# A hybrid attention and recurrence layer: shifting and centring the recurrent values through memory and with tokens on partitions, in place of 128 small products per run, and storing the last results block by block

## The chip, the cores and the metric

The kernel runs on one core of a Trainium2 chip. The metric is the device time of one execution in microseconds (us). Before the change it is 1977.34 us, the median of three runs between 1976.89 and 1977.49 us. The engines are named as the profile names them: PE is TensorE with its matrix products, PEld its weight loads, DVE is VectorE, ACT is ScalarE, POOL is GpSimd, SP is SyncE, whose queue issues nearly all transfers.

## What is computed

The layer projects 256 tokens of width 4096 once, and feeds two groups of heads and a gate from the result:

```python
proj = jnp.einsum('bsd,dc->bsc', x, w_in)
...
rw = rw_cols.astype(f32)
rw_prev = jnp.pad(rw, ((0, 0), (1, 0), (0, 0)))[:, :-1]
rw = rw + (rw_prev - rw) * mu_shift.astype(f32)
r, kr, vr, wd, ad = jnp.split(rw, _split_points(IN_SIZES[4:9]), axis=-1)
...
y = _rwkv7_scan(rh, decay.reshape(hs), kh, vh, -kk, kk * ah)
mu = jnp.mean(y, axis=-1, keepdims=True)
var = jnp.mean(jnp.square(y - mu), axis=-1, keepdims=True)
y = ((y - mu) * lax.rsqrt(var + GN_EPS)).reshape(B, S, RWKV_WIDTH) * gn_gain + gn_bias
bonus = jnp.sum(rh * kh * r_k, axis=-1, keepdims=True) * vh
rwkv_out = y + bonus.reshape(B, S, RWKV_WIDTH)

h = jnp.concatenate([fox_out, rwkv_out], axis=-1) * jax.nn.silu(z.astype(f32))
out = jnp.einsum('bsc,cd->bsd', h.astype(x.dtype), w_out)
x = _layernorm(ALPHA * x.astype(f32) + out.astype(f32), ln_gain, ln_bias, LN_EPS).astype(x.dtype)
```

The change is about `vr`, the values of the recurrence. Each of their 2048 columns is mixed with the same column one token earlier (the token shift). The scan writes `v_t k_t^T` into a state and reads that state, so its output is linear in the values. The kernel uses that: the mean over the 64 columns of a head, which the normalisation of `y` takes away, is taken away from the values ahead of the scan.

## The kernel before, in words

**Blocks.** The recurrent and attention heads are worked in eight pairs n, each of two groups of 128 columns. A pair has four blocks b of 512 projection columns. A block is 16 pieces of 512 KB of weights (`w_n_b_q`), and each piece is 12 products with 128x128 stationary and 128x512 moving operands: every float32 operand is split in a rounded part "h" and a rest "l", and three products are made of each (`mm`, L147 to L149). `fetch` (L214 to L218) issues the load of a piece on SP into one of four raw buffers `w`; ACT casts it to "h" (L141), DVE subtracts to get "l" (L142). There are four "h" buffers and three "l" buffers.

**What runs beside them.** All other work is written as generators, advanced by `slot` after every second step of a block. Code order thus sets the order of PE; for the other engines a scheduler orders the instructions by what it believes of their times, and each engine then runs its own list strictly in order. A wait of one instruction holds up all that stand behind it on its engine.

**The values.** Block b = 1 of a pair holds the values of the recurrence (256 columns of each of the two token halves m) and those of the attention. ACT copies the first to the tile `bk` (L807). `unload` turns them with products against the identity (`tr`, L722), so that columns lie on partitions and tokens run along the row; there the shift by one token is a shift along the row (`shifted`, `lerp`, L268 and L269), giving the tile `s2`, called `v` in `rwkv`. `rwkv` needs them the other way round again, with tokens on partitions, 64 to a chunk, and centred: L488 to L496 multiply `v` by the matrix `cent`, which turns and centres at once, into `vp`. ACT copies `vp` to the tiles `SV` and `UV` (L521, L522). `v` also goes into the bonus (`bon`, L524).

**What follows in a pair.** `gp` (L487) are the products of keys and queries of the chunks, masked by DVE to `gb` and `lt` (L507, L515). `gb` goes through memory (`nd`, L510) and comes back spread over all partitions (`Nb`, L511). Then DVE solves 32 small triangular systems row by row (L543, L546, tiles `prod` and `xc`), whose result goes through memory again (`td`, `T`, L552 to L554) and is turned into `X` (L559); only then come the products that read `SV` and `UV` (L575 onwards). POOL scales the keys by the chunk's decay (L490).

**The end.** After the last block of the output projection, the second token half is normalised block by block on DVE (L913) and on ACT (L944), and `store` (L907) issues the transfers of the result: two of two blocks each, then four of one block each.

Of the kernel before, what the change touches and what calls it, by code (L numbers as in the profile page):

```python
# [10 lines left out]
F32 = mybir.dt.float32  # L11
BF16 = mybir.dt.bfloat16
F32R = mybir.dt.float32r
AF = mybir.ActivationFunctionType
ALU = mybir.AluOpType
AX = mybir.AxisListType

P = 128
# [33 lines left out]
C_ID = 0  # L52
C_MASK = 128
C_ONES = 256
C_CENT = 384
C_E = 512
C_SCAN = 640
C_ROW = C_SCAN + S
C_W = C_ROW + 2
# [3 lines left out]
def constants():  # L63
    p = np.arange(P)[:, None]
    s = p % C
    t = np.arange(C)[None, :]
    cst = np.zeros((P, C_W), np.float32)
    cst[:, C_ID : C_ID + P] = np.eye(P)
    cst[:, C_MASK : C_MASK + C] = s < t
    cst[:, C_MASK + C : C_MASK + 2 * C] = s <= t  # L70
    same = (np.arange(P)[:, None] // HD) == (np.arange(P)[None, :] // HD)
    cst[:, C_ONES : C_ONES + P] = same
    cst[:, C_CENT : C_CENT + P] = np.eye(P) - same / HD
    j = (p % NG) * NJ + np.arange(P)[None, :] // B
    cst[:, C_E : C_E + P] = j == np.arange(P)[None, :] % B
    cst[:, C_SCAN : C_SCAN + S] = (np.arange(S)[None, :] % C) != 0
    first = np.array([1, 1, 0, 1, 0, 1], np.float32)
    sign = np.array([-1, -1, -1, 1, 1, 1], np.float32)
    cst[:6, C_ROW] = sign * (2 * first - 1)
    cst[:6, C_ROW + 1] = sign * (1 - first)  # L80
    return cst


@with_exitstack
def layer(ctx: ExitStack, tc: tile.TileContext, xt, xtok, w_lora, w_main, w_o, up, par, mulora, fbias, lng, lnb, cst, out):
    nc = tc.nc
    PS = bass.MemoryType.PSUM

# [6 lines left out]
    def pst(name):  # L95
        return ps.tile([P, 512], F32, tag="ps", name=name)
# [33 lines left out]

    ident = cs[:, C_ID : C_ID + P]
    ones = cs[:, C_ONES : C_ONES + P]
    cent = cs[:, C_CENT : C_CENT + P]

    def column(name, i):
        return prm[:, PAR.index(name), i : i + 1]
# [55 lines left out]
    def wait(n):  # L192
        for _ in range(n):
            yield
# [182 lines left out]
        return t.rearrange("p a b -> p (a b)")  # L377

    rk = {}
    pairs = {}  # L380
    done = set()
    prepared = set()
# [92 lines left out]
    def rwkv(n):  # L475
# [12 lines left out]
        v = vv[n]  # L488
        kept = BK[:, :, 0 : NCH - 1, :]
        nc.gpsimd.tensor_tensor(kept, kept, lc[:, :, 0 : NCH - 1].unsqueeze(3).to_broadcast([P, 2, NCH - 1, P]), ALU.mult)  # L490
        vp = pst(f"vp{n}")
        for u in range(2):
            for c in range(NCH):
                for j in range(2):
                    h, o = HALF[j], HALF[1 - j]
                    nc.tensor.matmul(vp[o, u * S + c * C : u * S + (c + 1) * C], v[:, u, c * C : (c + 1) * C], cent[:, h], start=True, stop=True)  # L496

        def m(rows):
            return cs[rows, C_MASK : C_MASK + P].unsqueeze(1).to_broadcast([C, NCH, P])

# [14 lines left out]
                nc.vector.tensor_tensor(lt[j][o, u], gv[u][j][o], m(o), ALU.mult)  # L515
        SV = [rp.tile([P, 2, NCH, C], F32, tag=f"SV{j}", name=f"SV{j}_{n}") for j in range(2)]
        UV = [rp.tile([P, 2, NCH, C], F32, tag=f"UV{j}", name=f"UV{j}_{n}") for j in range(2)]
        for j in range(2):
            o = HALF[1 - j]
            vo = vp.rearrange("p (u c t) -> p u c t", u=2, t=C)[o]  # L520
            nc.scalar.copy(SV[j][o], vo)  # L521
            nc.scalar.copy(UV[j][o], vo)  # L522
            nc.gpsimd.memset(SV[j][HALF[j], :, 0, :], 0.0)
        nc.vector.tensor_tensor(flat(bon), flat(bon), flat(v), ALU.mult)  # L524
        for u in range(2):
            nc.scalar.activation(bon[:, u], bon[:, u], AF.Identity, bias=column("gn_bias", i0 + u))
# [24 lines left out]
        for u in range(2):  # L551
            nc.sync.dma_start(out=td[u].rearrange("q c (g j) s -> (q c g) (j s)", g=NG), in_=flat(xc[:, u]))  # L552
            for a in range(4):
                nc.sync.dma_start(out=T[B * a : B * (a + 1), u], in_=td[u, a].rearrange("c r s -> r c s"))  # L554
        yield from wait(W["d2"])
        for a in range(4):
            o = C * (a // 2) + B * (a % 2)
            rows = slice(B * a, B * (a + 1))
# [146 lines left out]

    unloading = []

    def unload(n, b, bk, vt):
        yield from wait(LAG)
        if b == 0:  # L710
            while n and 2 * n - 1 not in prepared:
                yield
        elif b == 2:
            while n and n - 1 not in done:
                yield
        fq = fk = None
        cols = BLOCKS[b]
        for h in range(len(cols) // 2):
            tr = pst(f"tr{n}_{b}_{h}")
            for t in range(2):  # L720
                for m in range(2):
                    nc.tensor.transpose(tr[:, t * S + m * P : t * S + (m + 1) * P], bk[:, m, (2 * h + t) * P : (2 * h + t + 1) * P], ident)  # L722
            for t in range(2):
                p = tr[:, t * S : (t + 1) * S]
                j, u = cols[2 * h + t]
                i = 2 * n + u
                if j < 3:
                    rk[i, j] = shifted(p, j, i)
                elif j == 3:
                    while i and i - 1 not in foxed:  # L730
                        yield
                    fq = t256("fq", f"fq{i}")
                    nc.scalar.mul(fq, p, FOX_SCALE)
                elif j == 4:
                    fk = t256("fk", f"fk{i}")
                    nc.scalar.copy(fk, p)
                    side(fox(i, fq, fk, vt))
                else:
                    silu2(p, f"fr"[j - 5] + str(i))
            yield  # L740
        unloading.clear()
# [57 lines left out]
    for n in range(G // 2):  # L799
        for b in range(4):  # L800
            acc = block(n, b)
            while unloading:
                slot()
            bk = rp.tile([P, 2, OB], F32, tag="bk", name=f"bk{n}_{b}")
            for m in range(2):
                if b == 1:
                    nc.scalar.copy(bk[:, m, : 2 * P], acc[m][:, : 2 * P])  # L807
                else:
                    nc.scalar.copy(bk[:, m, :], acc[m])
            if b == 1:  # L810
                while n and 2 * n - 1 not in foxed:
                    slot()
                vt = rp.tile([P, 2, 2 * P], F32, tag="vt", name=f"vt{n}")
                for m in range(2):
                    nc.scalar.copy(vt[:, m, :], acc[m][:, 2 * P :])
            unloading.append(n)
            side(unload(n, b, bk, vt))
# [3 lines left out]
    for b, q in outs:  # L821
        if q == 0:
            pool, tag = (ps, "ps") if b == 1 or b and b % 2 == 0 else (pp, "pp")
            oacc[b] = [pool.tile([P, 512], F32, tag=tag, name=f"oacc{b}_{m}") for m in range(2)]
        acc = oacc[b]
        hi, lo = weights(f"wo{b}_{q}")
        for j in range(2):
            k = 2 * q + j
            if b < 2 and q < CUT:
                slot()  # L830
                if b == 0 and k + KT - BACK < FAR:
                    get_h(k + KT - BACK)
            while k not in ht:
                slot()
            if b > 1 and k == 4:
                load_tok(b)
            for m in range(2):
                if m and b == NB - 1 and q >= KT // 2 - LATE:
                    late.append((k, j, hi, lo))
                else:  # L840
                    project(acc[m], k, j, m, hi, lo)
        if q < KT // 2 - 1:
            continue
        if b == 0:
            while sides:
                slot()
            mid.close()
            rpool = ctx.enter_context(tc.tile_pool(name="rpool", bufs=1))
            res = [rpool.tile([P, D], F32, tag=f"res{m}", name=f"res{m}") for m in range(2)]
            rows = rpool.tile([P, D], F32R, name="rows")  # L850
            nc.gpsimd.memset(rows.bitcast(F32), 0.0)
            identr = const.tile([P, P], F32R, name="identr")
            nc.vector.tensor_copy(identr, ident)
            for n in range(2):
                load_tok(n)
            lneps = const.tile([P, 1], F32, name="lneps")
            nc.vector.memset(lneps, LN_EPS)
        if b < NB - 1:
            for m in range(2):
                add(m, b)  # L860
            for m in range(2):
                gain(m, b)
# [42 lines left out]
    def store(m, b, n):  # L905
        o = slice(b * OB, (b + n) * OB)
        nc.sync.dma_start(out=out[m * P : (m + 1) * P, o], in_=res[m][:, o])  # L907
# [31 lines left out]
    for n in range(HALVED):  # L939
        b = HALVED + n  # L940
        finish(1, b, l1, pp, "pp")
        o = slice(n * OB, (n + 1) * OB)
        nc.tensor.matmul(wps[n], la, rows[:, o], start=False, stop=True)
        nc.scalar.mul(res[1][:, o], wps[n], rss[1])  # L944
        if n == 1:
            store(1, 0, 2)
            store(1, HALVED, 2)
        elif n > 1:
            store(1, n, 1)
            store(1, b, 1)  # L950


def arrange(inputs):
# [12 lines left out]
    tiles = np.stack([t.reshape(KT, P, G // 2, 2, P) for t in types])  # L966
    main = np.stack([np.stack([tiles[j, :, :, :, u] for j, u in c], 3) for c in cols])
    res["w_main"] = np.ascontiguousarray(main.transpose(3, 0, 2, 1, 4, 5)).reshape(G // 2, 4, P, KT, OB)
    wo = a["w_out"].reshape(2, G, P, NB, OB)
    res["w_o"] = np.ascontiguousarray(wo.transpose(3, 2, 1, 0, 4).reshape(NB, P, KT, OB))  # L970
    res["up"] = np.ascontiguousarray(np.stack([a["w_up"].reshape(LORA, G, P).transpose(1, 0, 2), a["a_up"].reshape(LORA, G, P).transpose(1, 0, 2)], 2))
# [26 lines left out]
```

## Time and profile before

| what | value |
|---|---|
| median of three runs | 1977.34 us |
| the profiled execution's own time | 1977.29 us |
| its span in the trace | 1975.5 us |
| granted clock of PE over the span | 0.999 |
| PE, DVE, ACT, POOL busy | 99%, 67%, 51%, 2% |
| moved to and from memory | 387.64 MB, 196 GB/s |
| `vp` products in the trace | 256 records, 32 to a pair |
| POOL instructions | 86 |

The span is the time from the first to the last recorded instruction; the 1.8 us between it and the execution's own time lie outside the trace. Busy shares are averages over the span. Since one engine is busy nearly all of the time, the reading goes by that engine's list: what is taken off it, and what could make it wait.

### The profile page before, as it was taken

The numbers are of one execution on the slowest core, as the hardware profiler recorded it, in microseconds if no ns is written. First come the engines' busy times: TensorE is split into PE (matmuls) and PEld (weight loads), VectorE is DVE, ScalarE is ACT, GpSimd is POOL, SyncE is SP. The second block draws the span as 40 slices with busy tenths as digits, with TensorE's granted clock in tenths as the row PEclk, the third lists the DMA queues.
The fourth block names the chain that finished last, engine by engine and source line by source line (L and its number), as shares of the span: only waits on it lengthen the run. The fifth ranks groups of instructions, "written<-read, shape, count | busy, mean of one in ns | idle before, by whom it ended". The sixth has DMA issues, their size and how long they took to land.

```text
span 1975.5 us, 28732 instructions
## 1 busy us (share of the span) xinstructions
PE 1964.6 (99%) x10633; PEld 1615.7 (82%) x10633; DVE 1323.6 (67%) x2096; ACT 1007.9 (51%) x1525; POOL 37.7 (2%) x86
## 2 busy tenths in 40 slices
PE   9999999999999999999999999999999999999998
PEld 8888788878887888788878887888788878888886
DVE  6678576857685768576857685768576846755555
ACT  6554564456445644564456445644564444443332
POOL 0100000000000000000000000000000000000000
PEclk9999999999999999999999999999999999999999
DMA  9566566655665666566656665666566777866664
GB/s 336 150 198 179 178 191 199 189 166 192 199 185 169 193 193 187 173 193 192 184 177 192 198 186 170 190 195 189 171 186 184 244 281 235 253 199 201 190 202 161
DMA packets 140589, 387.64 MB, mean 196 GB/s; under 512 B 32224, under 2 KB 42480, under 8 KB 140448
## 3 DMA queue, kind: packets, MB, share of 16 engines
q1 hardware_dynamic: 140016, 385.38, 64.7%
q8 instruction: 83, 1.36, 0.3%
q14 instruction: 58, 0.48, 0.1%
q10 hardware_dynamic: 432, 0.43, 0.1%
HBM read 371.84 MB, written 13.91 MB: 195 GB/s over the span
## 4 chain that ended last, share of the span: by engine, by line
PE 99%; DVE 0%; ACT 0%; ACTq 0%; DVEq 0%; issue 0%
PE acc L147 24%; PE acc L149 24%; PE acc L148 24%; PE oacc L771 6%; PE oacc L773 6%; PE oacc L772 6%; PE tr L722 1%; PE yp L627 1%; PE gp L487 1%; PE up L602 1%; PE rh L575 1%; PE sp L611 0%; PE vp L496 0%; PE accl L149 0%; PE accl L147 0%; PE accl L148 0%
## 5 line engine op out<-in xcount | busy, mean ns | idle before, releaser
L546 DVE TENSOR_REDUCE xc<-prod 128x8 f32<-128x16 f32 (+30 forms) x248 | 73.1, 295 | 6.0
L543 DVE TENSOR_TENSOR prod<-Nb,xc 128x8 f32<-128x8 f32 (+30 forms) x248 | 72.3, 292 | 7.1
L142 DVE TENSOR_TENSOR w_9l<-w,w_9h 128x1024 fp32r<-128x1024 f32 x31 | 38.0, 1227 | 45.9 <-ACT pT L681 28.9
L142 DVE TENSOR_TENSOR w_1l<-w,w_1h 128x1024 fp32r<-128x1024 f32 x31 | 37.9, 1223 | 36.1 <-PE acc L149 36.1
L141 ACT CAST w_1h<-w 128x1024 fp32r<-128x1024 f32 x31 | 32.7, 1055 | 56.0 <-PE acc L148 39.7
L142 DVE TENSOR_TENSOR w_0l<-w,w_0h 128x1024 fp32r<-128x1024 f32 x31 | 37.9, 1223 | 33.8 <-PE acc L149 23.8
L142 DVE TENSOR_TENSOR w_3l<-w,w_3h 128x1024 fp32r<-128x1024 f32 x31 | 37.9, 1221 | 31.9 <-PE acc L149 31.8
L141 ACT CAST w_2h<-w 128x1024 fp32r<-128x1024 f32 x31 | 32.7, 1056 | 51.6 <-PE acc L148 47.1
L142 DVE TENSOR_TENSOR w_11l<-w,w_11h 128x1024 fp32r<-128x1024 f32 x31 | 37.9, 1223 | 31.5 <-PE acc L149 29.2
L142 DVE TENSOR_TENSOR w_6l<-w,w_6h 128x1024 fp32r<-128x1024 f32 x31 | 37.8, 1220 | 28.2 <-ACT UV L605 16.2
L141 ACT CAST w_11h<-w 128x1024 fp32r<-128x1024 f32 x31 | 32.6, 1051 | 45.9 <-PE acc L148 23.1
L141 ACT CAST w_13h<-w 128x1024 fp32r<-128x1024 f32 x31 | 32.7, 1054 | 45.1 <-PE acc L148 30.3
L142 DVE TENSOR_TENSOR w_10l<-w,w_10h 128x1024 fp32r<-128x1024 f32 x31 | 37.9, 1224 | 26.0 <-PE acc L149 25.8
L141 ACT CAST w_0h<-w 128x1024 fp32r<-128x1024 f32 x31 | 32.7, 1056 | 42.5 <-PE acc L148 40.9
L142 DVE TENSOR_TENSOR w_12l<-w,w_12h 128x1024 fp32r<-128x1024 f32 x31 | 37.5, 1209 | 23.6 <-PE acc L149 23.6
L147 PE MATMUL acc<-w_4h,x 128*128 128x512 f32 x124 | 53.0, 428 | 0.0
L142 DVE TENSOR_TENSOR w_15l<-w,w_15h 128x1024 fp32r<-128x1024 f32 x31 | 37.8, 1221 | 22.4 <-PE acc L149 20.9
L142 DVE TENSOR_TENSOR w_2l<-w,w_2h 128x1024 fp32r<-128x1024 f32 x31 | 37.9, 1222 | 22.3 <-PE acc L149 22.1
L141 ACT CAST w_15h<-w 128x1024 fp32r<-128x1024 f32 x31 | 32.6, 1051 | 37.6 <-PE acc L148 35.9
L141 ACT CAST w_14h<-w 128x1024 fp32r<-128x1024 f32 x31 | 32.7, 1054 | 36.7 <-PE acc L148 33.0
L147 PE MATMUL acc<-w_1h,x 128*128 128x512 f32 x124 | 51.2, 413 | 0.0
L147 PE MATMUL acc<-w_6h,x 128*128 128x512 f32 x124 | 51.2, 413 | 0.0
(833 smaller groups left out, 6570.3 us busy)
## 6 DMA issues: line engine op xcount, KB each, us to landing
w<-in_w_main_dram SPq DMA_DIRECT2D x496, 512.0 KB, 3.7
wo<-in_w_o_dram SPq DMA_DIRECT2D x128, 512.0 KB, 3.7
Nb<-nd SPq DMA_DIRECT2D x16, 512.0 KB, 5.5
wr<-in_w_main_dram SPq DMA_DIRECT2D x15, 512.0 KB, 5.8
hd<-hl SPq DMA_DIRECT2D x29, 256.0 KB, 4.5
h<-hd SPq DMA_DIRECT2D x29, 256.0 KB, 6.6
res<-in_xtok_dram SPq DMA_DIRECT2D x16, 256.0 KB, 4.6
xr<-in_xt_dram SPq DMA_DIRECT2D x15, 256.0 KB, 5.9
```

Of the source, the lines that this page charges most:

```text
L141: nc.scalar.copy(hi[:, :n], src[:, :n])
L142: nc.vector.tensor_tensor(lo[:, :n], src[:, :n], hi[:, :n].bitcast(F32), ALU.subtract)
L147: nc.tensor.matmul(acc[:, :n], xs[k][:, 0, tt], hi[:, o : o + n], start=(k == 0), stop=False)
L148: nc.tensor.matmul(acc[:, :n], xs[k][:, 1, tt], hi[:, o : o + n], start=False, stop=False)
L149: nc.tensor.matmul(acc[:, :n], xs[k][:, 0, tt], lo[:, o : o + n], start=False, stop=(k == KT - 1))
L487: nc.tensor.matmul(gp[u][j][:, c * P : (c + 1) * P], BK[h, u, c, :], lt[j][h, u, c, :], start=True, stop=True)
L543: first = nc.vector.tensor_tensor(prod[:, :, :, s + 1 :], nb[:, :, s : s + 1, s + 1 :].to_broadcast([P, 2, NJ, w]), xc[:, :, :, s + 1 :], ...
L546: nc.vector.tensor_reduce(xc[:, :, :, s : s + 1], prod[:, :, :, s:], AX.X, ALU.add)
L575: nc.tensor.matmul(rh[HALF[j], u * C : (u + 1) * C], lt[j][:, u, c, 0:C], SV[j][:, u, c, :], start=True, stop=True)
L771: nc.tensor.matmul(acc, ht[k][:, 0, tt], hi, start=(k == 0), stop=False)
L772: nc.tensor.matmul(acc, ht[k][:, 1, tt], hi, start=False, stop=False)
L773: nc.tensor.matmul(acc, ht[k][:, 0, tt], lo, start=False, stop=(k == KT - 1))
```

## The change

The products with `cent` and the matrix itself go. In their place, in block 1 of each pair, the copied columns `bk` are written to a buffer in memory (`vd`, one of two, whose first row is zero) from its second row on, and read back from its first row: the tile `vs` then holds, at each token's place, the token before. A row of shift coefficients (`muv`, prepared on the host) is loaded to all partitions, once a pair, into the buffer that later serves as `prod` and `T`. POOL does the mixing in three steps, `vs - bk`, times `muv`, plus `bk`. DVE sums each head's 64 columns to `vm`, and eight small instructions subtract the mean and place the chunks in `SV`; ACT copies `SV` to `UV`. The turned `v` is still made, for the bonus. The block loop may not copy block 2 of a pair to the single `bk` buffer until POOL's three steps stand in the code. At the end every block of the second half is stored by itself, DVE's block first.

```diff
 C_ONES = 256
-C_CENT = 384
-C_E = 512
+C_E = 384
...
         kept = BK[:, :, 0 : NCH - 1, :]
         nc.gpsimd.tensor_tensor(kept, kept, lc[:, :, 0 : NCH - 1].unsqueeze(3).to_broadcast([P, 2, NCH - 1, P]), ALU.mult)
-        vp = pst(f"vp{n}")
-        for u in range(2):
-            for c in range(NCH):
-                for j in range(2):
-                    h, o = HALF[j], HALF[1 - j]
-                    nc.tensor.matmul(vp[o, u * S + c * C : u * S + (c + 1) * C], v[:, u, c * C : (c + 1) * C], cent[:, h], start=True, stop=True)
-
+        p, t = bks[n], vs_[n]
+        nc.gpsimd.tensor_tensor(t, t, p, ALU.subtract)
+        nc.gpsimd.tensor_tensor(t, t, muvs[n].unsqueeze(1).to_broadcast([P, 2, 2 * P]), ALU.mult)
+        nc.gpsimd.tensor_tensor(t, t, p, ALU.add)
+        turned.add(n)
...
-        for j in range(2):
-            o = HALF[1 - j]
-            vo = vp.rearrange("p (u c t) -> p u c t", u=2, t=C)[o]
-            nc.scalar.copy(SV[j][o], vo)
-            nc.scalar.copy(UV[j][o], vo)
-            nc.gpsimd.memset(SV[j][HALF[j], :, 0, :], 0.0)
...
-        yield from wait(W["d2"])
+        vm = rp.tile([P, 2, 2, 2], F32, tag="vm", name=f"vm{n}")
+        vt = vs_[n].rearrange("p m (u j v) -> p m u j v", u=2, j=2)
+        nc.vector.tensor_reduce(vm.rearrange("p m u j -> p (m u j)"), vs_[n].rearrange("p m (a v) -> p (m a) v", v=HD), AX.X, ALU.add)
+        yield
+        for j in range(2):
+            o = HALF[1 - j]
+            for c in range(2):
+                h = HALF[c]
+                for a in range(2):
+                    nc.vector.scalar_tensor_tensor(
+                        SV[j][o, :, 2 * a + c, :], vm[h, a, :, j].unsqueeze(2).to_broadcast([C, 2, HD]), -1.0 / HD, vt[h, a, :, j, :], ALU.mult, ALU.add
+                    )
+            nc.scalar.copy(UV[j][o], SV[j][o])
+            nc.gpsimd.memset(SV[j][HALF[j], :, 0, :], 0.0)
+        yield from wait(W["d2"] - 1)
...
+    zero = rp.tile([1, 2 * P], F32, tag="prod", name="zero")
+    nc.gpsimd.memset(zero, 0.0)
+    vds = [dram.tile([S + 1, 2 * P], F32, name=f"vd{j}") for j in range(2)]
+    for vd in vds:
+        nc.sync.dma_start(out=vd[0:1], in_=zero)
...
-            while unloading:
+            while unloading or b == 2 and n not in turned:
                 slot()
...
+            if b == 0:
+                muvs[n] = rp.tile([P, 2 * P], F32, tag="prod", name=f"muv{n}")
+                nc.sync.dma_start(out=muvs[n], in_=muv[n : n + 1, :].to_broadcast([P, 2 * P]))
             if b == 1:
+                vd = vds[n % 2]
+                bks[n] = bk[:, :, : 2 * P]
+                nc.sync.dma_start(out=vd[1:].rearrange("(m p) c -> p m c", m=2), in_=bk[:, :, : 2 * P])
+                vs_[n] = rp.tile([P, 2, 2 * P], F32, tag="vs", name=f"vs{n}")
+                nc.sync.dma_start(out=vs_[n], in_=vd[:S].rearrange("(m p) c -> p m c", m=2))
...
-        if n == 1:
-            store(1, 0, 2)
-            store(1, HALVED, 2)
-        elif n > 1:
-            store(1, n, 1)
-            store(1, b, 1)
+        store(1, b, 1)
+        store(1, n, 1)
```

PE's list is the same row for row in both kernels, but for the `vp` rows that are gone. On three other engines it matters where the new rows stand. All pieces are of pair 3, block 2; a name such as `w_2_5l` is the rest of piece 5 of block 2, and the numbers at the end of names are buffers.

On DVE, between the bonus and piece 7, before:

```order
L524 TENSOR_TENSOR bon_6371<-bon_6371,s_6_6755 128x512
L142 TENSOR_TENSOR w_2_5l<-w_2_5_6784,w_2_5h 128x1024
L142 TENSOR_TENSOR w_2_6l<-w_2_6_6802,w_2_6h 128x1024
L507 TENSOR_TENSOR gb_838<-gp_0_0_6814,cs 64x512
L507 TENSOR_TENSOR gb_839<-gp_0_1_6815,cs 64x512
L515 TENSOR_TENSOR lt_3_6369<-gp_0_0_6814,cs 64x512
...
L515 TENSOR_TENSOR lt_3_6370<-gp_1_1_6817,cs 64x512
L142 TENSOR_TENSOR w_2_7l<-w_2_7_6891,w_2_7h 128x1024
```

The same place in the changed kernel:

```order
L517 TENSOR_TENSOR bon_6376<-bon_6376,s_6_6763 128x512
L550 TENSOR_REDUCE vm_7418<-vs_6721 128x8
L139 TENSOR_TENSOR w_2_5l<-w_2_5_6792,w_2_5h 128x1024
L557 SCALAR_TENSOR_TENSOR SV_3_6866<-vm_7418,vs_6721 64x2x64 x4
L557 SCALAR_TENSOR_TENSOR SV_3_6867<-vm_7418,vs_6721 64x2x64 x4
L139 TENSOR_TENSOR w_2_6l<-w_2_6_6810,w_2_6h 128x1024
L506 TENSOR_TENSOR gb_838<-gp_0_0_6822,cs 64x512
...
L514 TENSOR_TENSOR lt_3_6375<-gp_1_1_6825,cs 64x512
L139 TENSOR_TENSOR w_2_7l<-w_2_7_6879,w_2_7h 128x1024
```

The sum `vm` and the eight centring rows were written behind the solve in the code, but stand ahead of pieces 5 and 6 and of the eight masks; the solve comes after all of these.

On SP, the loads of the weights around the new transfers, in the changed kernel (before, only the `w` rows stand there, in the same order):

```order
L215 DMA w_2_4_6774<-in_w_main_dram 128x1024
L215 DMA w_2_5_6792<-in_w_main_dram 128x1024
L829 DMA vd_852<-bk_1_6717 128x2x256
L215 DMA w_2_6_6810<-in_w_main_dram 128x1024
L831 DMA vs_6721<-vd_852 128x2x256
L215 DMA w_2_7_6879<-in_w_main_dram 128x1024
L215 DMA w_2_8_6897<-in_w_main_dram 128x1024
```

The write `vd` stands between pieces 5 and 6, the read `vs`, which has to wait for it, between pieces 6 and 7. The load of `muv` of the next pair stands between pieces 5 and 6 of that pair's block 0.

On POOL, from the last small clearing before the pair's chunks to the first mask of the next attention head, in the changed kernel (before, the row of `BK` stands alone between `eL` and `nb`):

```order
L415 MEMSET eL_8010 128x4
L493 TENSOR_TENSOR vs_6721<-vs_6721,bk_1_6717 128x512
L494 TENSOR_TENSOR vs_6721<-vs_6721,muv_6321 128x512
L495 TENSOR_TENSOR vs_6721<-vs_6721,bk_1_6717 128x512
L491 TENSOR_TENSOR BK_6373<-BK_6373,lc_6372 128x2x384
L669 AFFINE_SELECT nb_7659<-nb_7659 128x128 x2
```

The three steps of the mixing stand ahead of the scaling of the keys.

More of the change, by code (lines that the diff above doesn't have):

```diff
@@ L72, in constants @@
     cst[:, C_ONES : C_ONES + P] = same
-    cst[:, C_CENT : C_CENT + P] = np.eye(P) - same / HD
     j = (p % NG) * NJ + np.arange(P)[None, :] // B
@@ L84, in layer @@
 @with_exitstack
-def layer(ctx: ExitStack, tc: tile.TileContext, xt, xtok, w_lora, w_main, w_o, up, par, mulora, fbias, lng, lnb, cst, out):
+def layer(ctx: ExitStack, tc: tile.TileContext, xt, xtok, w_lora, w_main, muv, w_o, up, par, mulora, fbias, lng, lnb, cst, out):
     nc = tc.nc
@@ L132, in layer @@
     ones = cs[:, C_ONES : C_ONES + P]
-    cent = cs[:, C_CENT : C_CENT + P]
     def column(name, i):
@@ L379, in layer @@
     rk = {}
+    vs_ = {}
+    bks = {}
+    muvs = {}
+    turned = set()
     pairs = {}
@@ L851, in layer @@
             nc.gpsimd.memset(rows.bitcast(F32), 0.0)
-            identr = const.tile([P, P], F32R, name="identr")
+            identr = rpool.tile([P, P], F32R, name="identr")
             nc.vector.tensor_copy(identr, ident)
@@ L968, in arrange @@
     res["w_main"] = np.ascontiguousarray(main.transpose(3, 0, 2, 1, 4, 5)).reshape(G // 2, 4, P, KT, OB)
+    res["muv"] = np.ascontiguousarray(a["mu_shift"][4096:6144].reshape(G // 2, 2 * P))
     wo = a["w_out"].reshape(2, G, P, NB, OB)
```

## The prediction

> **What bounds the kernel now.** I read the page first: busy shares, and the chain that ended last.
>
> ```profile
> span 1975.5 us, 28732 instructions
> PE 1964.6 (99%) x10633; PEld 1615.7 (82%) x10633; DVE 1323.6 (67%) x2096; ACT 1007.9 (51%) x1525; POOL 37.7 (2%) x86
> PE 99%; DVE 0%; ACT 0%; ACTq 0%; DVEq 0%; issue 0%
> ```
>
> The chain lies on PE for 99% of the span: PE never waits for long, so what is taken off its list comes off the end, as long as nothing new makes it wait. A gain is therefore not limited by what PE lets go, but by whether each piece of weights still reaches it in time. Next I read the chain in order of time, for the products that go. These are pair 3 and the last of the eight, pair 7, and pair 3 once more in PE's timeline:
>
> ```profile
> 727.80 1.08 PE vp L496 x32
> ...
> 1518.78 1.08 PE vp L496 x32
> ```
>
> ```profile
> 727.73 1.15 PE L496 MATMUL vp<-cs,s 128*64 128x64 f32 x32
> ```
>
> A pair's `vp` takes 1.08 us of the chain (1.15 from first start to last end, which overlaps with its neighbours), and the pairs repeat (1518.78 less 727.80 is four periods of 197.75 us), so I work out pair 3 and count it eight times.
>
> **Part 1, the products go.** 8 x 1.08 = 8.64 us come off PE. No other row of PE's list moves. The copies of `vp` on ACT go too and two come back from `SV`; ACT is at 51%, and none of it is on the chain.
>
> **Part 2, the new road of the values.** It is `bk`, `vd`, `vs`, three steps of POOL, `vm` and eight centring rows on DVE. The values themselves are not in a hurry: they are first read behind the solve. But `vm` stands in DVE's list ahead of the rests of pieces 5, 6 and 7, so if POOL is late, DVE waits at `vm` and PE waits for a piece. I need two times: T, when `vm` can start, and the latest T that PE doesn't feel.
>
> The start of the road is the second half of `bk`:
>
> ```profile
> 713.86 0.37 ACT L807 COPY bk<-acc 128x256 f32<-128x256 f32 x1
> ```
>
> It ends at 714.23, and `vd` is issued at 714.3. A write and a read of 256 KB so close together are not in the trace. These are the nearest transfers, from the page's list of issues (the last number is the median time to landing), and one load of a piece at that place:
>
> ```profile
> hd<-hl SPq DMA_DIRECT2D x29, 256.0 KB, 4.5
> h<-hd SPq DMA_DIRECT2D x29, 256.0 KB, 6.6
> res<-in_xtok_dram SPq DMA_DIRECT2D x16, 256.0 KB, 4.6
> ...
> nd<-gb SPq DMA_DIRECT2D x64, 16.0 KB, 2.0
> ```
>
> ```profile
> L218 SPq DMA_DIRECT2D w<-in_w_main_dram x1: 327/327/327, 714.4 to 714.4; - x1
> ```
>
> ```profile
> DMA to landing us min/median/max: 3.6/3.6/3.6
> ```
>
> The low end is 2.0 us each (16 KB), the high end 4.5 for the write and 6.6 for the read, which stand among other transfers. At 714.3 the queue is nearly empty: 512 KB land in 3.6 us. So I go along the line from 16 KB in 2.0 to 512 KB in 3.6: 256 KB take 2.0 + 1.6 x 240 / 496 = 2.8 us. `vd` lands at 717.1, `vs` is issued at 717.2 and lands at 720.0.
>
> POOL's price is in two views of its timeline, with DVE's beside the second:
>
> ```profile
> 727.68 1.47 POOL L490 TENSOR_TENSOR BK<-BK,lc 128x768 f32<-128x768 f32 x1 [37.54 <-DVE gb L507]
> ```
>
> ```profile
> 202.88 0.29 POOL L662 TENSOR_SCALAR_AFFINE_SELECT nb<-nb 128x128 f32<-128x128 f32 x1 [66.94 <-DMA nb<-ncd]
> 203.85 1.10 POOL L662 TENSOR_SCALAR_AFFINE_SELECT nb<-nb 128x128 f32<-128x128 f32 x1 [0.67 <-DMA nb<-ncd]
> ```
>
> ```profile
> 203.57 1.23 DVE L142 TENSOR_TENSOR w_14l<-w,w_14h 128x1024 fp32r<-128x1024 f32 x1 [1.49 <-PE acc L149]
> ```
>
> 768 columns take 1.47 us, so 512 take 0.98 and three steps 2.94. The same mask costs 0.29 us alone and 1.10 beside a DVE subtraction with two operands from SBUF, and it ends 0.15 us behind that (203.57 + 1.23 = 204.80): POOL stands still meanwhile. DVE at the new place:
>
> ```profile
> 719.04 1.23 DVE L142 TENSOR_TENSOR w_4l<-w,w_4h 128x1024 fp32r<-128x1024 f32 x1 [0.40 <-PE acc L149]
> ...
> 720.69 0.69 DVE L524 TENSOR_TENSOR bon<-bon,s 128x512 f32<-128x512 f32 x1
> 721.83 1.23 DVE L142 TENSOR_TENSOR w_5l<-w,w_5h 128x1024 fp32r<-128x1024 f32 x1 [0.45 <-PE acc L149]
> ...
> 726.94 1.41 DVE L507 TENSOR_TENSOR gb<-gp,cs 64x512 f32<-64x512 f32 x2 [1.16 <-PE gp L487]
> ...
> 732.46 1.21 DVE L142 TENSOR_TENSOR w_7l<-w,w_7h 128x1024 fp32r<-128x1024 f32 x1
> ```
>
> Piece 4's rest ends at 720.27, so POOL begins at 720.3; the bonus holds it up for another 0.69. T = 720.3 + 2.94 + 0.69 + 0.1 for hand-overs = 724.0. (With the low end of the transfers, POOL runs into piece 4's rest as well, and T only falls to 718.5 + 2.94 + 1.23 + 0.69 = 723.4.)
>
> Now the latest T. PE first needs piece 7's rest here:
>
> ```profile
> 737.15 0.39 PE L149 MATMUL acc<-w_7l,x 128*128 128x512 f32 x1
> ```
>
> Without `vp` that is 736.07. From `vm` to the end of that rest DVE has to do `vm` (128x512), pieces 5 and 6, eight centring rows, the masks and piece 7. Prices of `vm` and the centring by the nearest rows:
>
> ```profile
> 746.46 0.17 DVE L546 TENSOR_REDUCE xc<-prod 128x8 f32<-128x16 f32 x1
> ```
>
> ```profile
> 779.53 0.42 DVE L546 TENSOR_REDUCE xc<-prod 128x8 f32<-128x256 f32 x1
> ```
>
> ```profile
> L618 DVE TENSOR_TENSOR SV<-sp,sl x32: 275/288/297, 232.0 to 1622.0; 64x128 f32<-64x128 f32 x32
> ```
>
> A sum over 240 more columns costs 0.25 more, so 512 columns cost 0.69; eight rows of 64x128 cost 8 x 0.288 = 2.3; two rests 2.46; masks and piece 7 run from 726.94 to 733.67, 6.73. Together 12.18 us, so the latest T is 736.07 - 12.18 = 723.9. T is 0.1 later: PE waits 0.1 us a pair, 0.8 in all. The margin is thus used up to nothing; every further 0.1 us of T costs 0.8 us, and PE's gain is gone at a T of 723.9 + 1.08 = 725.0. One half microsecond of error on either side is what I allow the prices of POOL and DVE.
>
> [...]
>
> **Part 3, what else stands behind.** On SP, `vd` delays piece 6's load by some 0.3 us, and the wait of `vs` that of piece 7 by about 0.1. Piece 6, issued at 714.4, lands 3.6 us later (above), and its cast comes later still, so this is covered:
>
> ```profile
> 721.84 1.04 ACT L141 CAST w_6h<-w 128x1024 fp32r<-128x1024 f32 x1
> ```
>
> The cover is 721.84 - 718.0 = 3.8 us. `muv` of the next pair waits until `T` has been read by the transposes (and by small products behind them on PE), among the loads of that pair's block 0:
>
> ```profile
> 806.08 1.81 DVE L559 STREAM_TRANSPOSE X<-T 32x256 f32<-32x256 f32 x4
> ```
>
> They end at 807.89. Where `muv` stands in SP's time is not in this trace; but a load held up by a whole period of a piece, 721.83 - 719.04 = 2.8 us, would still be inside the 3.8. On ACT the refilling of `prod` now waits for POOL's second step, about 723, and piece 6's cast behind it ends near 725; PE needs it some 2.8 us ahead of piece 7, at about 733. POOL's scaling of the keys starts at 727.7 as before. The single `bk` is free at 724, long before block 2 is copied. The masks start 2.4 us later (T + 0.69 + 2.46 + 2.3 = 729.4 against 726.94), and with them `nd`, `Nb` and piece 11 behind these on SP, which is what is late next:
>
> ```profile
> 740.88 1.05 ACT L141 CAST w_11h<-w 128x1024 fp32r<-128x1024 f32 x1 [3.18 <-DMA w<-in_w_main_dram]
> ```
>
> ```profile
> 742.39 1.22 DVE L142 TENSOR_TENSOR w_11l<-w,w_11h 128x1024 fp32r<-128x1024 f32 x1 [1.50 <-PE acc L149]
> ```
>
> ```profile
> 748.03 0.39 PE L149 MATMUL acc<-w_11l,x 128*128 128x512 f32 x1
> ```
>
> Its rest ends at 743.61 and is needed at 748.03 - 1.08 = 746.95: 3.3 us of cover, of which 0.9 are left. Cost nothing, but no more than that.
>
> **Part 4, the end.** The views are the last rows of DVE and ACT, SP's stores, and the moved GB/s in slices of 0.2 us from 1967:
>
> ```profile
> 1966.15 2.72 DVE L913 SCALAR_TENSOR_TENSOR res<-res,rs,wp 128x512 f32<-128x512 f32 x4 [0.74 <-PE wp L912]
> ```
>
> ```profile
> 1967.67 4.26 SPq L907 DMA_DIRECT2D out_dram<-res  x6
> ```
>
> ```profile
> GB/s 0 0 0 0 0 0 0 266 369 451 389 410 389 389 430 430 369 389 430 389 277 410 410 369 389 399 399 328 399 399 369 369 420 369 82 0 0 0 0 0
> ```
>
> From 1968.4 to 1973.9 data flow without a gap: the end is set by when the first store starts and by 2.1 MB. The first is issued at 1967.67, when two blocks are ready on each engine; now it follows DVE's first block, 1966.15 + 2.72 / 4 = 1966.83. That is 0.8 us earlier; I take 0.7, for two more issues. The bounds are 0, if the later blocks set the end, and 0.8.
>
> **The sum**, against the profiled execution's 1977.29 us (0.05 below the median): 1977.29 - 8.64 + 0.8 - 0.7 = 1968.75, so 1968.8 us, 0.4% faster. A measurement of this kernel can tell about 0.2%, or 4 us, from no change.
>
> **The rivals.**
>
> *DVE's wait eats most of it.* Same mechanism, T between 724.4 and 725.0, since POOL, or the read behind piece 6, is half to one microsecond slower than I reckon. For it speaks that two of the five prices on the road are stretched from other sizes; against it, that once the bonus is over POOL has DVE's idle time to itself. PE then waits 0.5 to 1.1 us a pair: 1968.0 + 4 to 8.8, so 1972 to 1976.8 us.
>
> *Slower: the turn through memory is late.* If the write takes 4.5 us as `hd` did and the read 4.6 as `res` did, `vs` lands at 714.3 + 9.2 = 723.5 and T is 723.5 + 2.94 + 0.1 = 726.5, 2.6 us past the limit. Each pair loses 2.6 - 1.08 = 1.5 us: 1977.29 + 12.2 - 0.7 = 1988.8 us. It decides from T = 725.0 on, which is a turn of 7.7 us in place of my 5.7. Against it: those rows stood behind other transfers. [...]
>
> *The gain is not there.* What PE lets go is lost again at piece 11 or at the solve, and only the stores help: 1976.6 us. The 0.9 us of cover left at piece 11 speak against it.
>
> **How the numbers follow.** My forecast, with DVE's wait between nothing and 0.5 us a pair, has 0.58 (from 1977.29 - 8 x 1.15 - 0.8 = 1967.3, without a wait, to 1972); the eaten gain 0.20, the late turn 0.14, no gain 0.08. The range reaches over the first, second and fourth: 1967.3 to 1977.0 us. Faster by over 0.2% (below 1973.3) are the first and 0.14 of the second: 0.72. Within 0.2%: 0.06 and 0.08, so 0.14. Slower: 0.14.
>
> **What would show it.** In the profile of the changed kernel, `vm` should start 2.5 us or so behind the end of the bonus, released by POOL, and the rest of piece 7 end just before PE asks for it; PE's waits on that rest should sum to under 4 us. `vs` should land 5.7 us after `vd` is issued, and POOL's first step be stretched by the bonus. PE waiting for `w_7l` by over 1.1 us in each pair, or pieces 8 and 11 late, would make me wrong; so would a last store that ends no earlier after PE's last product than before.

## The result and the profile after

The changed kernel takes 1996.07 us, the median of four runs between 1994.46 and 2000.76, against 1977.41 us for the kernel before: a ratio of 1.0099 with a 95% interval of 1.0081 to 1.0117. It is slower by 1%; forecast was 0.4% faster. The profiled execution is the one of 1994.46 us.

The page of the changed kernel, its busy shares and its chain:

```profile
span 1992.7 us, 28327 instructions
PE 1967.0 (99%) x10377; PEld 1611.1 (81%) x10377; DVE 1356.3 (68%) x2168; ACT 999.1 (50%) x1509; POOL 72.6 (4%) x111
PE 45%; DMA 1%; DVE 1%; POOL 0%; ACT 0%; issue 0%; DVEq 0%; POOLq 0%; ACTq 0%; SPq 0%
```

PE has 256 records fewer, 32 in each pair: the 128 products with `cent`, each recorded twice. Yet it is busy for 2.4 us longer than before; POOL's 72.6 us are twice those of before. The chain no longer lies on PE alone; its shares add up to less than half of the span, so it was not followed to the start, and I take it only as a hint that something makes PE wait. The table of waits of PE (columns: total us, times, longest) says what:

```profile
PE acc L146 <- DVE w_7l L139: 15.4, 8, 2.1
PE tp L525 <- DVE lt L514: 0.4, 1, 0.4
PE acc L146 <- DVE w_6l L139: 0.3, 1, 0.3
```

Once in each of the eight pairs PE waits for the rest of piece 7 of block 2, the place that the prediction watched. From here on a time is that of pair 3. On the road of the values (ACT's, SP's, POOL's and DVE's timelines):

```profile
720.11 0.36 ACT L820 COPY bk<-acc 128x256 f32<-128x256 f32 x1
```

```profile
720.50 0.38 SPq L829 DMA_DIRECT2D vd<-bk  x1
```

```profile
722.81 0.38 SPq L831 DMA_DIRECT2D vs<-vd  x1
```

```profile
727.39 1.39 POOL L493 TENSOR_TENSOR vs<-vs,bk 128x512 f32<-128x512 f32 x1 [30.99 <-DMA vs<-vd]
728.86 1.29 POOL L494 TENSOR_TENSOR vs<-vs,muv 128x512 f32<-128x512 f32 x1
730.23 1.29 POOL L495 TENSOR_TENSOR vs<-vs,bk 128x512 f32<-128x512 f32 x1
733.93 1.60 POOL L491 TENSOR_TENSOR BK<-BK,lc 128x768 f32<-128x768 f32 x1 [2.40 <-PE gp L488]
```

```profile
726.95 0.69 DVE L517 TENSOR_TENSOR bon<-bon,s 128x512 f32<-128x512 f32 x1
731.56 0.69 DVE L550 TENSOR_REDUCE vm<-vs 128x8 f32<-128x512 f32 x1 [3.92 <-POOL vs L495]
732.16 1.22 DVE L139 TENSOR_TENSOR w_5l<-w,w_5h 128x1024 fp32r<-128x1024 f32 x1
733.41 3.29 DVE L557 SCALAR_TENSOR_TENSOR SV<-vm,vs 64x128 f32<-64x128 f32 x8
736.73 1.23 DVE L139 TENSOR_TENSOR w_6l<-w,w_6h 128x1024 fp32r<-128x1024 f32 x1
743.37 1.21 DVE L139 TENSOR_TENSOR w_7l<-w,w_7h 128x1024 fp32r<-128x1024 f32 x1
```

```profile
744.63 0.50 PE L146 MATMUL acc<-w_7l,x 128*128 128x512 f32 x1 [2.11 <-DVE w_7l L139]
```

DVE stands idle for 3.92 us at `vm`, T is 731.56, and the lateness runs through its list to the rest of piece 7. What the waits cost is more than the 15.4 us they last. This is the table of windows, 2 us each, one for each of the eight waits; seven lie behind the wait, that of 1346 begins within it (columns: PE, PEld, DVE, ACT, POOL busy, then the granted clock, DMA share and GB/s):

```profile
146.00:148.00 2.00, 2.00 (x7) 1.52 (x6) 0.78 (x1) 0.00 (x0) 0.00 (x0) 0.50 1.03 234
346.00:348.00 2.00, 2.00 (x11) 1.63 (x10) 1.54 (x2) 0.00 (x0) 0.00 (x0) 1.00 0.92 199
545.00:547.00 2.00, 2.00 (x6) 1.52 (x6) 1.14 (x2) 0.00 (x0) 0.00 (x0) 0.50 0.95 268
746.00:748.00 2.00, 2.00 (x6) 1.52 (x6) 0.85 (x1) 0.00 (x0) 0.00 (x0) 0.50 0.96 223
946.00:948.00 2.00, 2.00 (x10) 1.61 (x9) 1.55 (x2) 0.00 (x0) 0.00 (x0) 1.00 1.09 234
1146.00:1148.00 2.00, 2.00 (x6) 1.57 (x5) 1.24 (x2) 0.00 (x0) 0.00 (x0) 0.50 1.00 215
1346.00:1348.00 2.00, 1.24 (x5) 1.05 (x6) 2.00 (x3) 0.00 (x0) 0.00 (x0) 1.00 1.08 264
1547.00:1549.00 2.00, 2.00 (x11) 1.64 (x10) 1.55 (x2) 0.00 (x0) 0.00 (x0) 1.00 0.95 221
```

Behind four of the eight waits PE runs at half its clock (0.50) and gets 6 or 7 products done in 2 us in place of 10 or 11. Each such stretch lasts 3.41 us in the trace's clock records, so it costs half of that, some 1.7 us.

### The profile page after: what moved, and what is told of

Same layout as the page of the kernel before. It is cut to its first block, busy times and chain, and to the rows that moved or that the text cites. A ratio compares the mean times of both kernels' runs of the same rounds, so it can differ in the third digit from the quotient of the medians.

```text
span 1992.7 us, 28327 instructions
## 1 busy us (share of the span) xinstructions
PE 1967.0 (99%) x10377; PEld 1611.1 (81%) x10377; DVE 1356.3 (68%) x2168; ACT 999.1 (50%) x1509; POOL 72.6 (4%) x111
## 5 line engine op out<-in xcount | busy, mean ns | idle before, releaser
L146 PE MATMUL acc<-w_7l,x 128*128 128x512 f32 x124 | 51.8, 418 | 15.4 <-DVE w_7l L139 15.4
L144 PE MATMUL acc<-w_7h,x 128*128 128x512 f32 x124 | 51.6, 416 | 0.0
L138 ACT CAST w_4h<-w 128x1024 fp32r<-128x1024 f32 x31 | 32.7, 1055 | 36.8 <-PE acc L145 35.5
L144 PE MATMUL acc<-w_2h,x 128*128 128x512 f32 x124 | 51.1, 412 | 0.0
```

Source lines behind the costliest of these rows:

```text
L138: nc.scalar.copy(hi[:, :n], src[:, :n])
L144: nc.tensor.matmul(acc[:, :n], xs[k][:, 0, tt], hi[:, o : o + n], start=(k == 0), stop=False)
L146: nc.tensor.matmul(acc[:, :n], xs[k][:, 0, tt], lo[:, o : o + n], start=False, stop=(k == KT - 1))
```

## The experiments

The theory after the result: `vm` starts too late for the rest of piece 7, because several prices on its road were too low; PE's wait follows T and DVE's work behind `vm` one for one; and a wait of some 2 us can bring PE's clock down, which costs nearly as much again. The rivals: the new transfers and POOL's work cost PE or DVE time by their mere presence; the gain of the removed products was never there; the half clock has nothing to do with the waits. The kernel before, beside which they ran, took 1977.43 to 1977.64 us. Times are medians; the last two columns are counted in the one execution of each kernel that was profiled, which for the changed kernel was the fastest of four and for "less work on POOL" the slowest of ten (1983.75 us).

| kernel | us | ratio, 95% interval | PE's waits on `w_7l`, us (times) | half clock behind them |
|---|---|---|---|---|
| changed | 1996.07 | 1.0081 to 1.0117 | 15.4 (8) | 4 |
| sums and centring behind the solve | 1968.88 | 0.9943 to 0.9973 | none | 0 |
| centring alone behind the solve | 1970.19 | 0.9951 to 0.9977 | 0.7 (1) | 0 |
| before, products gone | 1969.44 | 0.9945 to 0.9975 | none | 0 |
| before, the road unread | 1977.12 | 0.9989 to 1.0008 | none | 0 |
| before, new stores | 1976.75 | 0.9986 to 1.0005 | none | 0 |
| changed, PE kept busy | 1992.50 | 1.0063 to 1.0093 | none | 0 |
| changed, read on POOL's queue | 2004.84 | 1.0118 to 1.0148 | 16.9 (8) | 8 |
| changed, read on ACT's queue | 2004.69 | 1.0124 to 1.0154 | 16.9 (8) | 7 |
| changed, read ahead of piece 6 | 1984.30 | 1.0020 to 1.0049 | 10.6 (8) | 1 |
| changed, less work on POOL | 1980.14 | 1.0006 to 1.0025 | 8.4 (7) | 1 |

**The waiting work moved behind.** The row sums and the eight centring rows are pinned to their place in the code, so that DVE issues them behind the solve, and ACT's copies to `UV` follow them. The lists of PE, POOL and SP are those of the changed kernel.

```diff
-        nc.vector.tensor_reduce(vm...)
+        tc.keep_in_program_order(nc.vector.tensor_reduce(vm...))
...
-                    nc.vector.scalar_tensor_tensor(SV[j][o, ...], vm[h, ...], ...)
+                    tc.keep_in_program_order(nc.vector.scalar_tensor_tensor(SV[j][o, ...], vm[h, ...], ...))
```

> Theory A (place): the change loses its time because the sum vm and the centring stand ahead of the rests of pieces 5 to 7 in DVE's list, so that DVE waits at vm for POOL, PE waits for piece 7, and PE's clock falls after some of these waits. Theory B (load): the new transfers and POOL's steps crowd the weights. Here vm and the eight centring rows are issued behind the solve, where the code has them; PE's, POOL's and SP's lists are those of the changed kernel row for row. A: no wait on piece 7 is left, granted clock as before, 1977.3 - 8.6 (products) - 0.9 (stores) = 1967.8 us, between 1967 and 1969. B: the same transfers still crowd, 1990 us or more.

It took 1968.88 us, faster than both kernels. All waits on `w_7l` are gone from the table of PE's waits, whose longest rows are now these three; the first two, at the end and at the start, are in the changed kernel too:

```profile
PE zp L921 <- DVE zd L909: 1.4, 1, 1.4
PE warmup L106 <- POOL idle L103: 1.3, 1, 1.3
PE oacc L786 <- DVE wo_3l L139: 0.8, 1, 0.8
```

POOL's steps go on beside DVE's work there (its second took 2.15 us), and `vm` and the centring are still in time for their readers. From one pair to the next (first `gp` to first `gp`) it needs 196.65 us, the kernel before 197.73: 1.08 less, what a pair's `vp` took. So the whole loss hangs on where two groups of instructions stand in DVE's list.

**The products alone gone.** The kernel before without `vp`; `SV` and `UV` are filled with the unturned `v`, so turning and centring are left out.

```diff
-        vp = pst(f"vp{n}")
-        ...
-            vo = vp.rearrange("p (u c t) -> p u c t", u=2, t=C)[o]
+            vo = v.rearrange("p u (c t) -> p u c t", t=C)[o]
```

> The kernel before without the products vp; SV and UV are copied from v as it lies, so the turning and centring of the values is left out, and nothing of the new road is there. Both theories: 1977.3 - 8 x 1.08 = 1968.7 us. If the products lay in time that PE would have lost anyway, 1977.

1969.44 us, and 196.66 us a pair. The gain of Part 1 is there in full, and the rival that it is not there falls.

**The road laid and not read.** The kernel before with `vd`, `vs`, `muv` and POOL's three steps, whose result nobody reads; `vp` stays.

```diff
+        nc.gpsimd.tensor_tensor(t, t, p, ALU.subtract)
+        nc.gpsimd.tensor_tensor(t, t, muvs[n]..., ALU.mult)
+        nc.gpsimd.tensor_tensor(t, t, p, ALU.add)
...
+                nc.sync.dma_start(out=vd[1:]..., in_=bk[:, :, : 2 * P])
+                nc.sync.dma_start(out=vs_[n], in_=vd[:S]...)
```

> The kernel before with the new road laid beside it: vd, vs, muv and POOL's three steps in every pair, at the same places of SP's and POOL's lists as in the change, but nobody on DVE reads the result, and the vp products stay. A: nothing waits for the road, 1977.3 us within 1. B: the transfers and POOL's steps are what costs, 1990 us or more.

1977.12 us, no change (0.9989 to 1.0008). The transfers and POOL's work cost nothing by themselves; only the wait for them does.

**PE kept busy.** Nine products that nobody reads stand ahead of piece 7 in each pair's block 2.

```diff
             hi, lo = weights(f"w{n}_{b}_{q}")
+            if b == 2 and q == 7:
+                keepw = pp.tile([P, 512], F32, tag="pp", name=f"keepw{n}")
+                for _ in range(9):
+                    nc.tensor.matmul(keepw, xs[0][:, 0, :P], hi[:, :OB], start=True, stop=True)
```

> The changed kernel with nine products more in each pair, ahead of piece 7's own, into a buffer that nobody reads: 9 x 0.227 = 2.04 us of PE work laid into the wait of 1.3 to 2.1 us. DVE's, ACT's, POOL's and SP's lists are the same row for row. If the price of the wait is only its length, the time stays at 1995 us or rises a little. If PE's idle time also throttles its clock (half clock in 4 stretches of 3.41 us in the changed kernel, 6.8 us in all), then the clock stays full here and the time falls by 6 to 9 us, to 1986 to 1989, although PE has more to do.

None of the eight places shows a half clock any more. Yet the time fell by only 3.6 us, to 1992.50, not by the 6 to 9 expected: nine products are 2.04 us in every pair, also where the wait had been 1.3 or 1.8, and new waits came with them:

```profile
PE fpt L690 <- DVE lg L686: 2.0, 2, 1.1
PE tp L529 <- DVE lt L518: 0.8, 2, 0.4
```

So the half clock hangs on the idle time, and filling that is a poor remedy: the filling costs what the wait did.

**The sums left early, the centring behind.** As in the first experiment, but `vm` stays where the changed kernel has it.

```diff
-                    nc.vector.scalar_tensor_tensor(SV[j][o, ...], vm[h, ...], ...)
+                    tc.keep_in_program_order(nc.vector.scalar_tensor_tensor(SV[j][o, ...], vm[h, ...], ...))
```

> The changed kernel with its row sums `vm` where they were, ahead of the rest of piece 7, and only the eight centring rows behind the solve; the lists of PE, POOL and SP stay. Theory (the lateness adds up: turn, POOL's steps and 3.3 us of centring ahead of the rest of piece 7): `vm` still starts about 11.1 us behind the end of block 1's copy, but the rest of piece 7 ends 3.3 us sooner, about a microsecond ahead of its first product, so PE's eight waits on it (15.4 us) go and with them the half clock: 1968 to 1971 us, near the 1968.88 of the kernel with both behind the solve. Rival (the wait at `vm` for POOL alone is the price): PE still waits about 2 us in each pair, 1990 us or more.

1970.19 us. `vm` starts 10.25 to 11.8 us behind the issue of `vd`, as late as before, and DVE still waits there; but in pair 3 the rest of piece 7 ends 9.57 us behind `vm`'s start in place of 13.02, and PE's waits for it are down to 0.7 us in all. The wait at `vm` alone is not the price: the 3.3 us of centring between it and piece 7 belong to it just as much.

**The read on another queue.** `vs` is read from POOL's queue, or from ACT's, in place of SP's, where piece 6's load stands ahead of it.

```diff
-                nc.sync.dma_start(out=vs_[n], in_=vd[:S]...)
+                nc.gpsimd.dma_start(out=vs_[n], in_=vd[:S]...)
```

> The changed kernel with the read of `vs` issued on POOL's queue in place of SP's; the lists of DVE, PE and ACT stay. Theory (the 4.6 us of the read are packets that stand behind piece 6's load in SP's queue): the read lands 1 to 1.5 us sooner, PE's waits on the rest of piece 7 fall from 15.4 us to some 5 to 8, few of them bring the half clock, 1977 to 1984 us. Rival (the engines' bandwidth is shared whatever the queue, or POOL's own issue costs as much): the read takes as long, the waits stay at 14 us or more, 1992 to 1998 us.

> The same with the read of `vs` on ACT's queue; the lists of PE, DVE and POOL stay. ACT then waits some 2.3 us for the write ahead of its next cast. Theory: as on POOL's queue, 1977 to 1984 us, if what ACT delays is covered. Rival: 1992 us or more, as the read is no faster or the casts behind ACT's wait come late.

Both made it worse, 2004.84 and 2004.69 us. From the issue of the read to POOL's first step it takes 3.3 to 5.4 us on POOL's queue and 3.5 to 5.9 on ACT's, where it took 3.3 to 5.2 on SP's. A place in SP's queue is therefore not what makes the read long. The theory's 1977 to 1984 us did not come, and for POOL's queue the rival's 1992 to 1998 was too low as well. With POOL's queue every wait is 2.11 or 2.12 us long, and now all eight are followed by a half clock. The wait on `w_7l` does not grow beyond that, although T lies up to 12.4 us behind the issue of `vd`: where T is that late, PE already stands still ahead of it, on `tp` for the last mask (2.1 us in all, six times) and on `w_6l` (0.6, twice). This is pair 3, in PE's timeline and the windows:

```profile
749.68 0.68 PE L146 MATMUL acc<-w_7l,x 128*128 128x512 f32 x1 [2.11 <-DVE w_7l L139]
```

```profile
750.00:753.00 3.00, 3.00 (x8) 2.35 (x8) 1.89 (x2) 0.00 (x0) 0.00 (x0) 0.50 1.00 227
```

A pair needs 201.38 us on the mean, 4.73 more than without the waits: 2.1 of wait, 1.7 of half clock, 0.3 on the mean for `tp` and `w_6l`, and 0.6 for the restart and the rest, which I did not divide further.

**The read ahead of piece 6.** SP holds piece 6's load until the read of `vs` has been issued; nothing else moves.

```diff
-            nc.sync.dma_start(out=raw, in_=src.rearrange("p k c -> p (k c)"))
+            with tc.issue_after(turn_[name].ins) if name in turn_ else ExitStack(): nc.sync.dma_start(out=raw, in_=src.rearrange("p k c -> p (k c)"))
...
-                nc.sync.dma_start(out=vs_[n], in_=vd[:S]...)
+                turn_[f'w{n}_2_6'] = nc.sync.dma_start(out=vs_[n], in_=vd[:S]...)
```

> The changed kernel with piece 6's load held on SP until the read of `vs` has been issued; every other engine's list stays. The read on another queue was no faster, so the queue is not what holds it. Theory (the read shares the DMA engines with the 512 KB of piece 6, issued 1.8 us ahead of it): with nothing ahead of it the read takes 2.8 to 3.5 us where it took 3.3 to 5.2, `vm` starts about 1 us sooner, and piece 6, 2.3 us later, is still cast in time; PE's waits on the rest of piece 7 fall from 15.4 us to 6 to 10, with no more than one or two half-clock stretches: 1976 to 1984 us. Rival (a read of what was just written takes some 4.5 us by itself): the waits stay at 14 us or more, 1992 us or more. A second rival: piece 6 becomes late, and PE waits for it in its place.

1984.30 us, and 10.6 us of waits: both just above what was expected. The read takes 2.7 to 2.9 us in all eight pairs, although the loads of pieces 6 and 7 now follow it, in pair 3 after 0.5 and 1.0 us. So it was the 512 KB of piece 6, issued 1.8 us ahead of it, that made it long. PE does not wait for piece 6, so the second rival falls as well. But T gained only 0.8 us, because POOL, which now starts beside DVE's work, is the slower for it:

```profile
725.26 2.15 POOL L493 TENSOR_TENSOR vs<-vs,bk 128x512 f32<-128x512 f32 x1 [29.12 <-ACT s L265]
727.48 1.61 POOL L494 TENSOR_TENSOR vs<-vs,muv 128x512 f32<-128x512 f32 x1
729.18 1.28 POOL L495 TENSOR_TENSOR vs<-vs,bk 128x512 f32<-128x512 f32 x1
```

```profile
725.03 1.22 DVE L139 TENSOR_TENSOR w_4l<-w,w_4h 128x1024 fp32r<-128x1024 f32 x1 [0.39 <-PE acc L146]
726.18 0.47 DVE L266 SCALAR_TENSOR_TENSOR s<-tr,prm,s 128x255 f32<-128x255 f32 x1
726.68 1.27 DVE L517 TENSOR_TENSOR bon<-bon,s 128x512 f32<-128x512 f32 x1
730.50 0.69 DVE L550 TENSOR_REDUCE vm<-vs 128x8 f32<-128x512 f32 x1 [2.54 <-POOL vs L495]
```

POOL's first step is drawn out from 1.29 to 2.15 us beside piece 4's rest, and the bonus from 0.69 to 1.27 beside POOL's first and second. PE's wait falls with T, and the clock stays up:

```profile
743.48 0.50 PE L146 MATMUL acc<-w_7l,x 128*128 128x512 f32 x1 [1.26 <-DVE w_7l L139]
```

```profile
744.00:746.00 2.00, 2.00 (x10) 1.59 (x10) 1.69 (x2) 0.00 (x0) 0.00 (x0) 1.00 1.02 219
```

Seven waits of 1.26 us brought no half clock; the eighth, in pair 0, lasted 1.79 and did.

**Less work on POOL.** POOL multiplies 32 columns by `muv` in place of 512, so the shift of the others is left out; only that step differs. (A second edit, not shown here, holds `vm` behind the bonus, its place in the changed kernel, so that DVE's list stays the same.)

```diff
-        nc.gpsimd.tensor_tensor(t, t, muvs[n].unsqueeze(1).to_broadcast([P, 2, 2 * P]), ALU.mult)
+        nc.gpsimd.tensor_tensor(t[:, :, :16], t[:, :, :16], muvs[n][:, :16].unsqueeze(1).to_broadcast([P, 2, 16]), ALU.mult)
```

> The changed kernel with POOL's multiplication by `muv` cut from 512 columns to 32; it leaves out the shift of the other columns. Only POOL's second step differs. Theory: `vm` starts 1.1 us sooner, PE's waits on the rest of piece 7 fall one for one, from 15.4 us to about 6.6, and since none is then over 1.3 us no wait brings the half clock: 1994.5 - 8.8 - 4 x 1.7 = 1978.9, so 1976 to 1980 us. Rival (the half clock hangs on the wait being there and not on its length): four stretches stay, 1985 to 1987 us.

1980.14 us, the median of ten between 1978.17 and 1983.75, just above the 1976 to 1980 expected. The waits are 8.4 us in place of 15.4, where 6.6 had been expected. They spread, since the read still varies from 3.5 to 5.2 us and T from 9.2 to 11.0 behind the issue of `vd`. The one wait of 2.12 us, in the pair with the latest T, is the only one with a half clock behind it; the six of 1.5 us or less have none. On the mean of the eight pairs POOL's three steps take 1.0 us less (3.33 against 4.31), T comes 1.1 us sooner, and PE waits 0.9 us less: nearly one for one, as the theory says.

**The stores alone.** The kernel before with the new order of the last stores.

```diff
-        if n == 1:
-            store(1, 0, 2)
-            store(1, HALVED, 2)
-        elif n > 1:
-            store(1, n, 1)
-            store(1, b, 1)
+        store(1, b, 1)
+        store(1, n, 1)
```

> The kernel before with the last stores of the changed one, block by block, and nothing else. Both theories: from PE's last product to the end 0.9 us less, 1976.4 us against 1977.3; a rival that the early stores gain more or less than the trace shows would give 1977.3 or under 1975.5.

1976.75 us, 0.7 under the kernel before on that chip; the interval (0.9986 to 1.0005) holds no change as well. The trace gives it more sharply: from the start of PE's last output product (`oacc`) to the end of the span it takes 13.4 us, before 14.2.

## Why the prediction was wrong, point by point

**The chain and Part 1: right.** 1.08 us a pair come off PE, and the end with it, once nothing makes PE wait: 196.65 against 197.73 us a pair, and 1968.88 us for the kernel with the centring behind the solve, where 1968.8 had been forecast for the changed one.

**Part 2: the place and the mechanism right, the sizes wrong; this is the step that failed.** "T is 0.1 later: PE waits 0.1 us a pair" was a difference of two long sums. Against pair 3, with the issue of `vd` as zero:

| term | predicted, us | measured, us |
|---|---|---|
| issue of `vd` to issue of `vs` | 2.9 | 2.31 |
| from there to POOL's start | 3.1 | 4.58 |
| POOL's three steps, with what holds them up | 3.63 | 4.14 |
| T | 9.7 | 11.06 |
| from `vm`'s start to the end of piece 7's rest | 12.18 | 13.02 |
| PE's first need of that rest | 21.77 | 22.02 |
| PE's wait | 0.1 | 2.1 |

Three terms carry it; the write, which was 0.6 us faster than forecast, took a part of them back. The read was taken at 2.8 us for an empty queue; the experiment that gave it one found just that, 2.7 to 2.9, but here piece 6's load had been issued 1.8 us earlier, so it took 4.58. The `res` row, 4.6 us among other transfers, was the nearer one. POOL's step was taken at 0.98 us, by columns from a scaling with 768; its true price alone is 1.29. The term as a whole is only 0.5 short, since the bonus, which was to hold POOL up for 0.69, drew its first step out by no more than 0.10 (1.39 against 1.29). The centring was taken at 8 x 0.288 us. Seven of the eight rows do take 0.28, and one takes 1.56:

```profile
L557 DVE SCALAR_TENSOR_TENSOR SV<-vm,vs x8: 278/284/1561, 733.4 to 736.4; 64x128 f32<-64x128 f32 x8
```

It stands beside POOL's scaling of the keys, 733.93 to 735.53 above. I had reckoned what DVE does to POOL, and not what POOL does to DVE at the later place. The half microsecond of error that I allowed was too little for a sum of so many prices, several of them stretched from other sizes.

**The price of a wait: missing.** "Every further 0.1 us of T costs 0.8 us" holds only up to waits of some 1.8 us: one of 1.71 us brought no half clock, those of 1.79 and 1.82 did. Behind four waits the half clock took 4 x 1.7 = 6.8 us more (half of 3.41 each), and no row of before could show that, since PE never waited for longer than 1.4 us there.

**Part 3 and Part 4: right.** Piece 11, on which 0.9 us of cover had been left, is not in PE's waits. The stores gained 0.9 us from the start of PE's last output product to the end of the span (14.19 to 13.26), 0.7 were forecast.

**The sum.** The span grew by 1992.7 - 1975.5 = 17.2 us: -8.6 for the products, +16.9 for the eight waits (15.4, and some 0.2 at each restart), +6.8 for the half clock, -0.9 for the stores, and +3.0 that remain. Of these 0.7 are the waits on `tp` and `w_6l`, 0.5 are a longer output projection (363.1 against 362.6 us from its first product to its last), and the cause of 1.8 stays open. The wait on `wo_3l` of the kernel with the centring behind the solve is not in the changed kernel. All this is the profiled execution, the fastest of four; the others took 0.3 to 6.3 us more, at a granted clock of 0.993 to 0.996, and have no trace.

**The rivals.** The nearest was "the turn through memory is late", which had 0.14. Its T of 726.5 was 12.2 us behind the issue of `vd`, measured were 11.06; its 1988.8 us are about what the changed kernel would take without the half clock, 1994.5 - 6.8 = 1987.7. That is in part luck. Its read was right (4.6 us, measured 4.58), and the evidence that I set against it, that those rows stood behind other transfers, was the evidence for it: so does this read. But its write was not late (4.5 us, measured 2.31); POOL's steps and the centring, which it took at my prices, made up for most of that.

## What to carry to other kernels

Where an instruction that waits for a long road stands in an in-order list ahead of work that the bound engine needs, and nobody needs its result yet, put it behind that work: here this turned 1.0% slower into 0.4% faster, with the same work. When a forecast rests on a margin of 0.1 us between two sums of ten, take every transfer from a row that has the same neighbours, count contention in both directions (here up to 0.9 us on a step of POOL beside DVE, and 1.3 on a row of DVE beside POOL), and put the error of the sum, not a hope, into the range. And once the bound engine idles for some 2 us, ask for its granted clock behind the wait before pricing the wait at its length: here 2.1 us of wait brought up to 1.7 us more.

## What the runs showed of the hardware

- **PE's clock fell after idle times of 1.8 to 2.1 us, though not after every one.** Waits of 2.1 us brought a stretch of 3.41 us at half clock in all eight pairs with the read on POOL's queue, in seven of eight with the read on ACT's, and in three of five such pairs of the changed kernel; 1.79 and 1.82 us did once each, 1.71 and all of 1.49 or less did not. The four stretches of the changed kernel start at 144.80, 544.16, 745.55 and 1144.91 us, whole multiples of 3.413 us apart. I laid steps of 3.413 us through these starts and took the longest part of each wait that lies within one step: for the eight waits of the changed kernel it comes to 1.82 to 2.12 us where the clock fell and to 1.26 to 1.81 where it did not, so near 1.8 us it goes both ways; the three waits of 2.1 us that brought nothing, its own two and the one with ACT's queue, lie across the edge of two steps. So in these runs the place of a wait counts beside its length; how the clock comes to fall was not shown. With the read on POOL's queue a pair takes 201.38 us, 59 such steps, and the wait comes to lie at nearly the same place of a step in every pair; its eight waits are not eight independent trials.
- **POOL and DVE held each other up.** A centring row of 0.28 us took 1.44 to 1.60 beside POOL's scaling in each of the eight pairs of the changed kernel; in pair 3 it ran from 734.12 to 735.68, so it started 0.19 us behind the scaling and ended 0.15 us behind it. With the read ahead of piece 6 a step of POOL took 2.15 us in place of 1.29 beside a rest of DVE, and the bonus on DVE 1.27 in place of 0.69 beside POOL's steps.
- **What else was in flight set the time of this read, not its queue.** In the changed kernel the write of 256 KB released the read after 2.2 to 3.1 us; the read of the same 256 KB, up to POOL's first step, took 3.3 to 5.2 us behind a load of 512 KB in its own queue; in the other runs it took 2.7 to 2.9 when no load had been issued between the write and it, and 3.3 to 5.9 from another queue with that load issued ahead of it.
